# Seven block products for the first four heads' values and gates in a two-layer decoder trunk

## The chip, the core and the metric

The kernel runs on one core of a Trainium2 chip. The metric is the device time of one execution in microseconds (us); less is better. The core's engines run in parallel, each through its own instruction queue in order: TensorE (PE in the profile, with its weight loads PEld), VectorE (DVE), ScalarE (ACT), GpSimd (POOL), and SyncE (SP), which here issues the DMAs. Semaphores order them. PE multiplies a stationary 128x128 tile by a moving tile of up to 512 columns and accumulates in PSUM; the other engines move PSUM to SBUF.

## The reference

One sequence of 512 tokens, width 1024, two layers. Layer 0 mixes tokens with a Mamba-2 recurrence, layer 1 with HGRN2; each is followed by a squared-ReLU MLP (width 4096), layer norms, and a gated embedding. What this change touches is the input of the HGRN2 mixer, with 8 heads of 128 columns:

```python
q, fz, v, g = jnp.split(u @ w_in, 4, axis=-1)          # u: 512 x 1024, w_in: 1024 x 4096
...
o = rms_norm(o, norm_w).reshape(bsz, seq, D_MODEL) * jax.nn.silu(g)
```

`v` are the values that the recurrence carries, `g` the gates that scale its output. All is float32.

## The kernel before

Each float32 operand is split into a high part (rounded to fp32r, made by ACT) and a low part (the difference, made by DVE), and each product is three matmuls, `mm3` (lines 117 to 120): high x high, high x low, low x high. A weight block of 128x1024 comes by DMA into one of three `raw` buffers; `unit` and `split` (lines 101 to 115) make its two parts, in one of six slots each (`whi`, `wlo`). A new split can start only when the matmuls that read its slot are done.

Layer 0's MLP already uses block products with sums. Two operands are cut into 2x2 blocks, and seven products of sums of blocks stand for eight products of blocks (Winograd's form of Strassen's method). `weight_sums` (line 314) makes the four sums of weights on DVE, in eight buffers named `r`; `half_blocks` makes the sums on the other side; `block_product` (line 335) runs the seven products and drains them into `acc`.

After the MLP, `mlp_and_gate` multiplies the tokens by gate weights, chunk by chunk (4 chunks of 128 tokens, 2 halves of 512 columns), and adds the gated embedding. `turn` (line 441) then transposes each finished tile on PE, and its high and low parts go to `x_n`: ACT makes the high part (L449), DVE the low one (L450). The last tile's turn is left over in `late` and is run a little later. `x_n` is the transposed token matrix on which all of HGRN2's projections work.

The projections are made by generators. `vg(i)` (line 780) multiplies by the value and gate weights of heads 2i and 2i+1 (four weight blocks, 4 chunks x 8 x 3 = 96 matmuls of 512 columns) and drains to two `res` tiles, values and gates, from the pool `w4` (two buffers for each of the tags a and b). `qf(h)` makes query and forget gate of head h (48 matmuls). `background()` (line 839) strings them together, with `out0`, half of the output projection; every step of it is three matmuls and counts 0.65.

The recurrence `hcore` (line 877) runs for a pair of heads. It has seven levels, m = 0 to 6 (`half` = 1 to 64), each with small matmuls on PE (L897, L911, L918), then products on DVE (L931, L932) that the next level needs, and copies into the score tile on ACT (L954, L960); then transposes (L967) and a copy (L969), states (L976 to L980), outputs (L989, L991), norm and gate (L996 to L1002), and transposes (L1009). After each it yields a credit from `FILL`, and `fill` runs as many background steps as the credit pays, so that PE has work while the other engines compute. The last pair's credits are scaled by `LAST`. PE's order in this stage is as written; on the other engines and elsewhere a scheduler orders by priority, which `tc.high_priority(offset=...)` raises. What is left of the second output projection follows by the scheduler and can also be put between.

At the start of this stage the background runs 16 steps of `vg(0)`, the late turn in between, then `qf(0)` and `qf(1)`, and `AHEAD` pays for some more.

Of the kernel before, what the change touches and what calls it, by code (L numbers as in the profile page):

```python
# [29 lines left out]
SOON = 40  # L30
# [8 lines left out]
FIRST_V = 8  # L39
CONSTS = dict(ident=P, triu=P, eps=1, convw=96, convb=24, dskip=16, snw=16, dtc=2, hlb=8, hnw=1)  # L40


# [1 line left out]
def trunk(ctx: ExitStack, tc, a):  # L44
    nc = tc.nc
    pool = lambda name, bufs, **kw: ctx.enter_context(tc.tile_pool(name=name, bufs=bufs, **kw))
    cpool = pool("consts", 1)
    raws = pool("raws", RAWS)
    whip = pool("whip", 6)
    wlop = pool("wlop", 6)  # L50
    b8 = pool("b8", 9)
    accp = pool("accp", 1)
    w4 = pool("w4", 2)
    sm = pool("sm", 2)
    pad = pool("pad", 1)
    psj = pool("psj", 4, space=PSUM)
    pst = pool("pst", 1, space=PSUM)
    psy = pool("psy", 1, space=PSUM)
# [42 lines left out]
    def unit(src, lead=LEAD):  # L101
        n = src.shape[1]
        with tc.high_priority(offset=lead):
            raw = mk(raws, [P, 1024], "raw")
            nc.sync.dma_start(raw[:, :n], src)
        return split(raw[:, :n], lead)

    def split(f, lead=LEAD):
        n = f.shape[1]
        with tc.high_priority(offset=lead):  # L110
            hi = mk(whip, [P, 1024], "whi", F32R)
            nc.scalar.copy(hi[:, :n], f)  # L112
            lo = mk(wlop, [P, 1024], "wlo", F32R)
            nc.vector.tensor_sub(lo[:, :n], f, f32(hi[:, :n]))  # L114
        return hi, lo

    def mm3(out, sh, sl, mh, ml, start, stop, **kw):
        nc.tensor.matmul(out, sh, mh, start=start, stop=False, **kw)  # L118
        nc.tensor.matmul(out, sh, ml, start=False, stop=False, **kw)  # L119
        nc.tensor.matmul(out, sl, mh, start=False, stop=stop, **kw)  # L120
# [26 lines left out]
    with tc.high_priority(offset=FIRST):  # L147
        idle = tmp("sq", [P, T])
        nc.vector.memset(idle, 0.0)
        ps = bank(psm, "pm")  # L150
# [3 lines left out]
    x_s = Split(8)  # L154
    four = [(mk(whip, [P, 2, T], "whi", F32R), mk(wlop, [P, 2, T], "wlo", F32R)) for _ in range(4)]
    with tc.high_priority(offset=FIRST):
# [7 lines left out]
        for k in range(8):  # L164
            hi, lo = (v[:, k % 2, :] for v in four[k // 2])
# [145 lines left out]
        put("s1", a22)  # L311
        put("s4", a12)

    def weight_sums(w, lead):

        t = [[None, None] for _ in range(4)]

        def load(i, u, src):
            t[i][u] = tmp("r", [P, 1024])
            nc.sync.dma_start(t[i][u], src)  # L320

        with tc.high_priority(offset=lead):
            for u in range(2):
                load(0, u, w[0][1][u])
                load(2, u, w[1][1][u])
                nc.vector.tensor_sub(t[2][u], t[2][u], t[0][u])
                load(1, u, w[0][0][u])
                nc.vector.tensor_sub(t[0][u], t[0][u], t[1][u])
                nc.vector.tensor_add(t[1][u], t[2][u], t[1][u])
            for u in range(2):  # L330
                load(3, u, w[1][0][u])
                nc.vector.tensor_sub(t[3][u], t[3][u], t[1][u])
        return t

    def block_product(w, blk, lead, first, after=None, turns=None, sums=None):
# [49 lines left out]
    def mlp_and_gate(layer, h_s, last):  # L385
# [35 lines left out]
        for g, period in enumerate(PERIODS):  # L421
            if g < 4:
                tiles = hidden(g)
            if g > 0:
                if g == 4:
                    h_s, after, turned, sums = norm(2 * layer + 1)
# [6 lines left out]
                w = [[[w2[8 * g - 8 + 4 * i + 2 * j + u] for u in range(2)] for j in range(2)] for i in range(2)]  # L433
# [2 lines left out]
                next(tiles if op == "T" else products)  # L436

        x_n = None if last else Split(8)
        late = []

        def turn(h, c):

            sl = slice(c * P, (c + 1) * P)
            pt = bank(pst, "pt")
            for j in range(4):
                nc.tensor.transpose(pt[:, j * P : (j + 1) * P], acc[:, c, h * 512 + j * P : h * 512 + (j + 1) * P], ident)
            v = pt.rearrange("p (j t) -> p j t", j=4)
            hh = x_n.hi[h][:, :, sl]
            nc.scalar.copy(hh, v)  # L449
            nc.vector.tensor_sub(x_n.lo[h][:, :, sl], v, f32(hh))  # L450

        pps = {}
# [9 lines left out]
        for h in range(2):  # L462
            pu = unit(a[f"wp_{layer}"][h])
            gu = [unit(a[f"wg_{layer}"][4 * h + j]) for j in range(4)]
            for c in range(NCH):
                sl = slice(c * P, (c + 1) * P)
# [18 lines left out]
                for i in range(2 if end else 1):  # L485
# [7 lines left out]
                    d = acc[:, c, fs]  # L493
# [7 lines left out]
        return x_n, late  # L501

    ps = bank(psj, "pj")
# [23 lines left out]
    ab = row("xs")  # L529
# [220 lines left out]
    g, s, ss = outs.pop(0)  # L750
    ssd_out(g, s, rms_group(ss), *after)
    begin("mlp0")
    x_s, late = mlp_and_gate(0, h_s, False)
# [26 lines left out]
    def vg(i):  # L780


        pss = {}
        units = []
        res = [mk(w4, [P, NCH, 256], "ab"[which]) for which in range(2)]
        for j, c in ((j, c) for j in range(4) for c in range(NCH)) if i else ((j, c) for c in range(NCH) for j in range(4)):
            if j == len(units):
                units.append(unit(a["whvg"][4 * i + j]))
            if j == 0:
                pss[c] = bank(psj, "pj")  # L790
            hi, lo = units[j]
            sl = slice(c * P, (c + 1) * P)
            for k in range(2):
                ks = slice(k * 512, (k + 1) * 512)
                x = x_s.h(2 * j + k, sl), x_s.l(2 * j + k, sl)
                mm3(pss[c], *x, hi[:, ks], lo[:, ks], j + k == 0, j == 3 and k == 1)
                yield 0.65
            if j == 3:
                for which in range(2):
                    nc.scalar.copy(res[which][:, c, :], pss[c][:, 256 * which : 256 * (which + 1)])  # L800
        nc.scalar.activation(res[1], res[1], AF.Silu)
        made["vg", i] = res

    def qf(h):
# [48 lines left out]
    made = {}  # L853
# [23 lines left out]
    def hcore(h0, s, i0):  # L877

        R = range(2)
        base = lambda half: 0 if half == 32 else 128  # L880
        vs = [slice(r * P, (r + 1) * P) for r in R]
# [82 lines left out]
        for r in R:  # L964
# [3 lines left out]
            kt.append(tmp("btok", [P, 3, P]))  # L968
            nc.scalar.copy(kt[r], pt[:, : 3 * P].rearrange("p (c k) -> p c k", c=3))  # L969
            yield FILL[1]  # L970
        v, sg = need("vg", h0 // 2)
        sv = []
        for r in R:
            pss = py(1) if r else bank(psm, "pm")
            for c in range(3):
                nc.tensor.matmul(pss[:, c * P : (c + 1) * P], kt[r][:, c, :], v[:, c, vs[r]], start=True, stop=True)  # L976
            sv.append(tmp("pv", [P, 3, P]))
            nc.scalar.copy(sv[r][:, 0], pss[:, 0:P])
            for c in range(1, 3):
                nc.vector.scalar_tensor_tensor(  # L980
                    sv[r][:, c], sv[r][:, c - 1], tot[r][:, c : c + 1], pss[:, c * P : (c + 1) * P], ALU.mult, ALU.add
                )
            yield FILL[2]
        os = []
        for r in R:
            po = py(r)
            for c in range(NCH):
                sl = slice(c * P, (c + 1) * P)
                nc.tensor.matmul(po[:, sl], scs[r][:, c, :], v[:, c, vs[r]], start=True, stop=c == 0)  # L989
                if c:  # L990
                    nc.tensor.matmul(po[:, sl], qd[r][:, sl], sv[r][:, c - 1, :], start=False, stop=True)  # L991

            ms = mk(sm, [P, NCH], "hms")
            o = tmp("cbm", [P, NCH, P])
            for c in range(NCH):
                nc.scalar.activation(o[:, c, :], po[:, c * P : (c + 1) * P], AF.Square, accum_out=ms[:, c : c + 1])  # L996
            nc.scalar.activation(ms, ms, AF.Sqrt, scale=1.0 / P, bias=eps)
            ri = mk(sm, [P, NCH], "hri")
            nc.vector.reciprocal(ri, ms)
            for c in range(NCH):  # L1000
                nc.vector.scalar_tensor_tensor(
                    o[:, c, :], po[:, c * P : (c + 1) * P], ri[:, c : c + 1], sg[:, c, vs[r]], ALU.mult, ALU.mult  # L1002
                )
            os.append(o)
            yield FILL[3]
# [144 lines left out]
```

## Time and profile before

| | us |
|---|---|
| median of 3 runs (lowest, highest) | 1431.18 (1430.93, 1432.43) |
| span of the profiled execution | 1430.3 |
| PE, PEld busy in it | 1422.1, 1180.6 |
| DVE, ACT, POOL busy in it | 1011.7, 735.0, 1.9 |

The profile is of one execution; its own time is not listed beside the runs, and its span is what lies between its first and last instruction, 0.9 under the median. A row of the timeline gives start and length in us, engine, line and operation, the tile written and the tiles read, shapes, and in brackets the idle time before it and what ended that. A row of a group gives count, busy time in all, mean in ns of one, and idle time before with its releasers. A matmul's length is pipelined and modelled, so its cost is read from the distance of the starts.

In the profiled execution the MLP of layer 0 ends at some 705 us, the gated embedding at some 766, and the first level of the recurrence begins at 807.7; its last level starts at 1000.1.

### The profile page before, as it was taken

To read this page: it belongs to the slowest core of one execution; us is meant where nothing else is said; L and a number is where in the kernel's file an instruction comes from. 1 tells how busy PE (TensorE), PEld (TensorE's weight loads), DVE (VectorE), ACT (ScalarE), POOL (GpSimd) and SP (SyncE) were. 2 spreads that over 40 slices of the span, in tenths; PEclk is the share of its full clock that TensorE was granted. 3 is DMA by queue.
4 is the path that set the end of the run, shared out by engine and by line. 5 is a ranking of instruction groups with operands and counts; after the bars stand their busy time and mean duration, and the time that the engine had idled before them with its cause. 6 is when DMAs were issued, how large, how long until landed. Compare 5 with 4: busy or idle time off the path is not lost.

```text
span 1430.3 us, 20978 instructions
## 1 busy us (share of the span) xinstructions
PE 1422.1 (99%) x8405; PEld 1180.6 (83%) x8405; DVE 1011.7 (71%) x1636; ACT 735.0 (51%) x1113; POOL 1.9 (0%) x12
## 2 busy tenths in 40 slices
PE   9999999999999999999999999999999999999998
PEld 7788888888888888888888887887898888888887
DVE  7988687797967667687853555556685867667873
ACT  6776454563264444545533465554555454544641
POOL 0000000000000000000000000000000000000000
PEclk9999999999999999999999999999999999999999
DMA  8332323233333444442422322122163434434231
GB/s 305 133 131 91 119 88 120 102 117 127 140 118 133 147 143 138 147 135 101 162 77 74 119 75 89 62 88 96 49 232 113 147 132 148 146 133 162 89 118 44
DMA packets 48529, 174.88 MB, mean 122 GB/s; under 512 B 5424, under 2 KB 6192, under 8 KB 48304
## 3 DMA queue, kind: packets, MB, share of 16 engines
q1 hardware_dynamic: 48432, 173.55, 34.8%
q8 instruction: 66, 1.08, 0.3%
q14 instruction: 31, 0.25, 0.1%
HBM read 171.36 MB, written 2.16 MB: 121 GB/s over the span
## 4 chain that ended last, share of the span: by engine, by line
PE 96%; DVE 2%; ACT 1%; DMA 0%; issue 0%; SPq 0%; DVEq 0%; ACTq 0%
PE pj L118 25%; PE pj L119 24%; PE pj L120 24%; PE py L118 5%; PE py L119 5%; PE py L120 5%; PE py L674 1%; PE py L680 1%; PE pm L644 1%; PE py L911 1%; PE pt L232 1%; DVE wlo L114 1%; PE pt L632 1%; PE py L989 0%; DMA r<-in_w 0%; PE py L991 0%
## 5 line engine op out<-in xcount | busy, mean ns | idle before, releaser
L112 ACT CAST whi<-raw 128x1024 fp32r<-128x1024 f32 x224 | 234.9, 1051 | 340.1 <-PE pj L119 240.0
L118 PE MATMUL pj<-b,whi 128*128 128x512 f32 (+1 forms) x1006 | 382.6, 381 | 0.7 <-ACT b L236 0.7
L119 PE MATMUL pj<-b,whi 128*128 128x512 f32 (+1 forms) x1006 | 381.0, 379 | 0.5 <-DVE b L237 0.5
L114 DVE TENSOR_TENSOR wlo<-raw,whi 128x1024 fp32r<-128x1024 f32 x224 | 272.5, 1222 | 153.4 <-ACT whi L112 150.5
L120 PE MATMUL pj<-b,wlo 128*128 128x512 f32 (+1 forms) x1006 | 379.7, 378 | 0.0
L118 PE MATMUL pj<-whi,b 128*128 128x512 f32 x576 | 230.1, 400 | 0.0
L120 PE MATMUL pj<-whi,b 128*128 128x512 f32 x584 | 228.7, 392 | 0.0
L119 PE MATMUL pj<-wlo,b 128*128 128x512 f32 x576 | 226.1, 393 | 0.0
L118 PEld LDWEIGHTS pj<-b,whi 128*128 128x128 f32 x1006 | 189.2, 188 | 34.3 <-ACT b L236 0.9
L119 PEld LDWEIGHTS pj<-b,whi 128*128 128x128 f32 x1006 | 189.8, 189 | 33.4 <-issue 0.9
L120 PEld LDWEIGHTS pj<-b,wlo 128*128 128x128 f32 x1006 | 189.6, 189 | 33.4
L120 PEld LDWEIGHTS pj<-whi,b 128*128 128x128 f32 x584 | 109.7, 188 | 22.5
L118 PEld LDWEIGHTS pj<-whi,b 128*128 128x128 f32 x576 | 108.4, 188 | 21.6 <-ACT b L1010 0.6
L119 PEld LDWEIGHTS pj<-wlo,b 128*128 128x128 f32 x576 | 108.5, 188 | 20.2
L112 ACT CAST whi<-r 128x1024 fp32r<-128x1024 f32 x64 | 67.4, 1054 | 63.7 <-PE pj L120 35.6
L114 DVE TENSOR_TENSOR wlo<-r,whi 128x1024 fp32r<-128x1024 f32 x64 | 78.1, 1221 | 21.6 <-ACT whi L112 21.4
L120 PE MATMUL py<-whi,b 128*128 128x512 f32 (+1 forms) x218 | 84.6, 388 | 0.0
L119 PE MATMUL py<-wlo,b 128*128 128x512 f32 x192 | 74.8, 390 | 0.0
L118 PE MATMUL py<-whi,b 128*128 128x512 f32 x192 | 74.5, 390 | 0.0
L573 DVE SCALAR_TENSOR_TENSOR cv<-pj,cst,cv 128x509 f32<-128x509 f32 (+2 forms) x66 | 48.7, 745 | 3.5 <-ACT cv L570 2.8
L120 PEld LDWEIGHTS py<-whi,b 128*128 128x128 f32 x218 | 41.0, 188 | 8.4
L931 DVE TENSOR_TENSOR cv<-cv,y 128x256 f32<-128x256 f32 x48 | 20.2, 422 | 33.0 <-PE py L911 20.4
(260 smaller groups left out, 1809.6 us busy)
## 6 DMA issues: line engine op xcount, KB each, us to landing
raw<-in_w SPq DMA_DIRECT2D x112, 512.0 KB, 3.2
r<-in_w SPq DMA_DIRECT2D x64, 512.0 KB, 3.4
raw<-in_wssd SPq DMA_DIRECT2D x36, 512.0 KB, 3.4
a<-csd SPq DMA_DIRECT2D x16, 512.0 KB, 3.7
raw<-in_wso SPq DMA_DIRECT2D x16, 512.0 KB, 3.2
raw<-in_wg SPq DMA_DIRECT2D x16, 512.0 KB, 3.3
raw<-in_whvg SPq DMA_DIRECT2D x16, 512.0 KB, 3.3
raw<-in_whq SPq DMA_DIRECT2D x16, 512.0 KB, 3.3
```

Source lines behind the costliest of these rows:

```text
L112: nc.scalar.copy(hi[:, :n], f)
L114: nc.vector.tensor_sub(lo[:, :n], f, f32(hi[:, :n]))
L118: nc.tensor.matmul(out, sh, mh, start=start, stop=False, **kw)
L119: nc.tensor.matmul(out, sh, ml, start=False, stop=False, **kw)
L120: nc.tensor.matmul(out, sl, mh, start=False, stop=stop, **kw)
L232: nc.tensor.transpose(pt[:, j * P : (j + 1) * P], src[:, k * P : (k + 1) * P], ident)
L573: nc.vector.scalar_tensor_tensor(cv[:, d:], ps[:, : T - d], convw[:, i, k : k + 1], cv[:, d:], ALU.mult, ALU.add)
L632: nc.tensor.transpose(pt[:, c * P : (c + 1) * P], xs[:, c * P : (c + 1) * P], ident)
L644: nc.tensor.matmul(pst_[:, c * P : (c + 1) * P], btok[:, c, :], xw[:, c].rearrange("p h q -> p (h q)"), start=True, stop=True)
L674: nc.tensor.matmul(yd[64 * r : 64 * r + 64, sl], xdt[:, 2 * c + r, :], m[:, r, sl], start=True, stop=True)
L680: nc.tensor.matmul(yo[:, c * P : (c + 1) * P], pv[:, c - 1].rearrange("p h q -> p (h q)"), cm[:, c * P : (c + 1) * P], start=True, stop=True,)
L931: nc.vector.tensor_mul(kv[:, :, 0, :], kv[:, :, 0, :], bc(tv[:, :, 1], 2, half))
```

## The change

The values and gates of heads 0 to 3 (`vg(0)` and `vg(1)`) are no longer made in the background. A new function, `values4`, makes them in one go directly after the gated embedding, with seven block products: tokens 0 to 255 and 256 to 511 by the two halves of the 1024 inner columns on one side, the same inner halves by heads 0 and 1 and heads 2 and 3 on the other. Each product is 2 chunks x 4 x 3 = 24 matmuls.

- The sums of weights come from `weight_sums`, now with an engine as argument: GpSimd here, with priority raised by 300, so that its loads and sums are placed early, towards the end of the MLP. Eight loads and eight operations of 128x1024. Six more weight blocks are loaded again and used as they are.
- The sums of transposed tokens need the tokens in float32: `turn` copies each transposed tile once more on ACT, into `rows`. DVE forms four sums, and each is split (`put`) into high and low parts in a `b8` buffer.
- The order of the products is: part (0,0); [late turn]; part (0,1); s3 with the third weight sum; s2 with the second; part (1,1) with the fourth; s1 with the first; s4. "Product three" below is the one on s3. The drains are copies on ACT (`first`) or additions on DVE (`more`).
- The background loses `vg(0)` and `vg(1)`; the credits in `FILL` are scaled down; `res` tiles now hold values and gates of two chunks each; the mask's load goes to a `raw` buffer in place of a `w4` one.

```diff
-JOBS = "q2 q3 v1 q4 q5 v2 q6 q7 v3 o".split()
-FILL = (3.7, 1.3, 1.6, 2.3, 2.8)
+JOBS = "q2 q3 q4 q5 v2 q6 q7 v3 o".split()
+FILL = (3.15, 1.1, 1.35, 1.95, 2.4)
+VALUE_SUMS = 300
...
-    def weight_sums(w, lead):
+    def weight_sums(w, lead, eng=nc.vector):
...
-                nc.vector.tensor_sub(t[2][u], t[2][u], t[0][u])
+                eng.tensor_sub(t[2][u], t[2][u], t[0][u])
...
         x_n = None if last else Split(8)
+        rows = None if last else [tmp("blk", [P, 2, 4, 256]) for _ in range(2)]
...
             nc.scalar.copy(hh, v)
+            nc.scalar.copy(rows[c // 2][:, h, :, c % 2 * P : (c % 2 + 1) * P], v)
             nc.vector.tensor_sub(x_n.lo[h][:, :, sl], v, f32(hh))
...
+    def values4(xs, rows, late):
+
+        w = [[[a["whvg"][4 * j + 2 * i + u] for u in range(2)] for j in range(2)] for i in range(2)]
+        t1, t2, t3, t4 = weight_sums(w, VALUE_SUMS, nc.gpsimd)
+        a11, a12, a21, a22 = (rows[i][:, j] for i in range(2) for j in range(2))
+        res = [[mk(w4, [P, 2, T], "ab"[i]) for i in range(2)] for _ in range(2)]
+
+        def put(f):
+            t = mk(b8, [P, 2, 4, 256], "b8", F32R)
+            nc.scalar.copy(t[:, 0], f)
+            nc.vector.tensor_sub(t[:, 1], f, f32(t[:, 0]))
+            return lambda k, c: tuple(t[:, i, k, c * P : (c + 1) * P] for i in range(2))
...
+        def product(x, us, banks, start, drain):
+            for c in range(2):
+                for k in range(4):
+                    hi, lo = us[k // 2]
+                    ks = slice(k % 2 * T, (k % 2 + 1) * T)
+                    mm3(banks[c], *x(k, c), hi[:, ks], lo[:, ks], start and k == 0, k == 3, skip_group_check=True)
+                with tc.high_priority(offset=SOON):
+                    drain(c, banks[c])
...
+        product(part(0, 0), [unit(v) for v in w[0][0]], x, True, first(0, 0))
+        for f in late:
+            f()
+        nc.vector.tensor_add(a22, a21, a22)
+        nc.vector.tensor_sub(a21, a11, a21)
+        s3 = put(a21)
+        product(part(0, 1), [unit(v) for v in w[1][0]], z, True, more(0, 0))
+        nc.vector.tensor_sub(a11, a22, a11)
+        s2 = put(a11)
+        product(s3, sums(t3), y, True, first(1, 1))
+        product(s2, sums(t2), x, False, first(1, 0))
+        s1 = put(a22)
+        product(part(1, 1), sums(t4), y, False, more(1, 0))
+        nc.vector.tensor_sub(a12, a12, a11)
+        s4 = put(a12)
+        product(s1, sums(t1), x, False, more(1, 1))
+        product(s4, [unit(v) for v in w[1][1]], x, False, first(0, 1))
+        for j in range(2):
+            for i in range(2):
+                g = res[j][i][:, :, 256:]
+                nc.scalar.activation(g, g, AF.Silu)
+            made["vg", j] = res[j]
...
+    with tc.manual_schedule(engines={mybir.EngineType.PE}):
+        values4(x_s, rows, late)
     begin("hgrn")
...
-    lmf = mk(w4, [P, 6, 32], "a")
+    lmf = mk(raws, [P, 1024], "raw")[:, :192].rearrange("p (m l) -> p m l", m=6)
...
-        first = vg(0)
-        for _ in range(FIRST_V):
-            yield next(first)
-        for f in late:
-            f()
-        for _ in range(FIRST_V):
-            yield next(first)
         yield from qf(0)
         yield from qf(1)
-        yield from first
```

More of the change, by code (lines that the diff above doesn't have):

```diff
@@ L33 @@
 SUMS = (60, 300, 300, 300)
-JOBS = "q2 q3 v1 q4 q5 v2 q6 q7 v3 o".split()
-FILL = (3.7, 1.3, 1.6, 2.3, 2.8)
+JOBS = "q2 q3 q4 q5 v2 q6 q7 v3 o".split()
+FILL = (3.15, 1.1, 1.35, 1.95, 2.4)
+VALUE_SUMS = 300
 AHEAD = 6.0
 LAST = 0.78
-FIRST_V = 8
 CONSTS = dict(ident=P, triu=P, eps=1, convw=96, convb=24, dskip=16, snw=16, dtc=2, hlb=8, hnw=1)
@@ L325, in weight_sums @@
                 load(2, u, w[1][1][u])
-                nc.vector.tensor_sub(t[2][u], t[2][u], t[0][u])
+                eng.tensor_sub(t[2][u], t[2][u], t[0][u])
                 load(1, u, w[0][0][u])
-                nc.vector.tensor_sub(t[0][u], t[0][u], t[1][u])
-                nc.vector.tensor_add(t[1][u], t[2][u], t[1][u])
+                eng.tensor_sub(t[0][u], t[0][u], t[1][u])
+                eng.tensor_add(t[1][u], t[2][u], t[1][u])
             for u in range(2):
                 load(3, u, w[1][0][u])
-                nc.vector.tensor_sub(t[3][u], t[3][u], t[1][u])
+                eng.tensor_sub(t[3][u], t[3][u], t[1][u])
         return t
@@ L500, in mlp_and_gate, with part, first, more @@
                     late.append(lambda h=h, c=c: turn(h, c))
-        return x_n, late
+        return x_n, rows, late
+    def values4(xs, rows, late):
[8 more added lines that the diff above has]
+            return lambda k, c: tuple(t[:, i, k, c * P : (c + 1) * P] for i in range(2))
+        def part(i, j):
+            sl = lambda c: slice((2 * i + c) * P, (2 * i + c + 1) * P)
+            return lambda k, c: (xs.h(4 * j + k, sl(c)), xs.l(4 * j + k, sl(c)))
+        def product(x, us, banks, start, drain):
[6 more added lines that the diff above has]
+                    drain(c, banks[c])
+        def first(i, j):
+            return lambda c, ps: nc.scalar.copy(res[j][i][:, c], ps)
+        def more(i, j):
+            return lambda c, ps: nc.vector.tensor_add(res[j][i][:, c], ps, res[j][i][:, c])
+        pair = lambda: [bank(psj, "pj") for _ in range(2)]
+        sums = lambda t: [split(v) for v in t]
+        x, z, y = [bank(psy, "py%d" % c) for c in range(2)], pair(), pair()
+        product(part(0, 0), [unit(v) for v in w[0][0]], x, True, first(0, 0))
[20 more added lines that the diff above has]
+            made["vg", j] = res[j]
@@ L752, in trunk @@
     begin("mlp0")
-    x_s, late = mlp_and_gate(0, h_s, False)
+    x_s, rows, late = mlp_and_gate(0, h_s, False)
+    made = {}
+    with tc.manual_schedule(engines={mybir.EngineType.PE}):
+        values4(x_s, rows, late)
     begin("hgrn")
     lmask = mk(cpool, [P, 6, 32], "lmask", U8)
-    lmf = mk(w4, [P, 6, 32], "a")
+    lmf = mk(raws, [P, 1024], "raw")[:, :192].rearrange("p (m l) -> p m l", m=6)
     nc.sync.dma_start(lmf, a["lmask"])
@@ L784, in vg @@
         units = []
-        res = [mk(w4, [P, NCH, 256], "ab"[which]) for which in range(2)]
-        for j, c in ((j, c) for j in range(4) for c in range(NCH)) if i else ((j, c) for c in range(NCH) for j in range(4)):
+        res = [mk(w4, [P, 2, T], "ab"[half]) for half in range(2)]
+        for j, c in ((j, c) for j in range(4) for c in range(NCH)):
             if j == len(units):
@@ L798, in vg @@
             if j == 3:
-                for which in range(2):
-                    nc.scalar.copy(res[which][:, c, :], pss[c][:, 256 * which : 256 * (which + 1)])
-        nc.scalar.activation(res[1], res[1], AF.Silu)
+                nc.scalar.copy(res[c // 2][:, c % 2], pss[c])
+        for r in res:
+            nc.scalar.activation(r[:, :, 256:], r[:, :, 256:], AF.Silu)
         made["vg", i] = res
@@ L839, in background @@
     def background():
-        first = vg(0)
-        for _ in range(FIRST_V):
-            yield next(first)
-        for f in late:
-            f()
-        for _ in range(FIRST_V):
-            yield next(first)
         yield from qf(0)
         yield from qf(1)
-        yield from first
         for job in JOBS:
             yield from {"v": vg, "q": qf}[job[0]](int(job[1])) if job != "o" else out0()
-    made = {}
     bg = background()
@@ L880, in hcore @@
         base = lambda half: 0 if half == 32 else 128
-        vs = [slice(r * P, (r + 1) * P) for r in R]
         q, f, kk = ([need("qf", h0 + r)[n] for r in R] for n in range(3))
@@ L970, in hcore @@
             yield FILL[1]
-        v, sg = need("vg", h0 // 2)
+        res = need("vg", h0 // 2)
+        v = lambda c, r: res[c // 2][:, c % 2, r * P : (r + 1) * P]
+        sg = lambda c, r: res[c // 2][:, c % 2, 256 + r * P : 256 + (r + 1) * P]
         sv = []
@@ L975, in hcore @@
             for c in range(3):
-                nc.tensor.matmul(pss[:, c * P : (c + 1) * P], kt[r][:, c, :], v[:, c, vs[r]], start=True, stop=True)
+                nc.tensor.matmul(pss[:, c * P : (c + 1) * P], kt[r][:, c, :], v(c, r), start=True, stop=True)
             sv.append(tmp("pv", [P, 3, P]))
@@ L988, in hcore @@
                 sl = slice(c * P, (c + 1) * P)
-                nc.tensor.matmul(po[:, sl], scs[r][:, c, :], v[:, c, vs[r]], start=True, stop=c == 0)
+                nc.tensor.matmul(po[:, sl], scs[r][:, c, :], v(c, r), start=True, stop=c == 0)
                 if c:
@@ L1001, in hcore @@
                 nc.vector.scalar_tensor_tensor(
-                    o[:, c, :], po[:, c * P : (c + 1) * P], ri[:, c : c + 1], sg[:, c, vs[r]], ALU.mult, ALU.mult
+                    o[:, c, :], po[:, c * P : (c + 1) * P], ri[:, c : c + 1], sg(c, r), ALU.mult, ALU.mult
                 )
```

## The prediction

> **What bounds the kernel now.** I read the page first: its first part, then the chain that ended last. TensorE (PE) has work in 1422.1 of 1430.3 us, and 96% of the chain is PE.
>
> ```profile
> span 1430.3 us, 20978 instructions
> PE 1422.1 (99%) x8405; PEld 1180.6 (83%) x8405; DVE 1011.7 (71%) x1636; ACT 735.0 (51%) x1113; POOL 1.9 (0%) x12
> ...
> PE 96%; DVE 2%; ACT 1%; DMA 0%; issue 0%; SPq 0%; DVEq 0%; ACTq 0%
> ```
>
> So the time is the sum of PE's instructions plus its waits: a removed matmul counts in full, and so does a new wait of PE. Next comes the timeline of PE where the changed stage begins. (Columns: start, length, engine, line.) These rows are the second and the last of the 24 matmuls ahead of the last turned tile, the four transposes, and the next matmul.
>
> ```profile
> 767.15 0.39 PE L119 MATMUL pj<-wlo,b 128*128 128x512 f32 x1
> ...
> 772.16 0.39 PE L120 MATMUL pj<-whi,b 128*128 128x512 f32 x1
> 772.39 0.60 PE L446 MATMUL pt<-cst,acc 128*128 128x128 f32 x4
> 772.75 0.48 PE L118 MATMUL pj<-whi,b 128*128 128x512 f32 x1
> ```
>
> A row's length, 0.39, is pipelined; what a 128x512 matmul costs is the distance of starts: 22 steps in 5.01 us, 0.228 each. For the other engines I take the groups by shape (mean ns of one behind the bar), and one hand-over from PE to ACT to DVE:
>
> ```profile
> L112 ACT CAST whi<-raw 128x1024 fp32r<-128x1024 f32 x224 | 234.9, 1051 | 340.1 <-PE pj L119 240.0 <-PE pj L120 72.0 <-PE py L120 20.7
> L114 DVE TENSOR_TENSOR wlo<-raw,whi 128x1024 fp32r<-128x1024 f32 x224 | 272.5, 1222 | 153.4 <-ACT whi L112 150.5 <-DMA r<-in_w 2.0
> L332 DVE TENSOR_TENSOR r<-r,r 128x1024 f32<-128x1024 f32 x16 | 19.6, 1222 | 7.7 <-DMA r<-in_w 7.6
> L365 DVE TENSOR_TENSOR acc<-py,acc 128x512 f32<-128x512 f32 x44 | 30.1, 687 | 6.5 <-PE py L120 6.5
> L449 ACT CAST b<-pt 128x512 fp32r<-128x512 f32 x8 | 4.7, 585 | 1.5 <-PE pt L446 1.5
> L800 ACT COPY a<-pj 128x256 f32<-128x256 f32 x16 | 6.0, 372 | 20.0 <-PE pj L120 20.0
> ```
>
> ```profile
> 758.98 0.39 PE L120 MATMUL pj<-whi,b 128*128 128x512 f32 x1
> 759.40 0.60 ACT L484 ACTIVATE sg<-pj 128x512 f32<-128x512 f32 x1 [6.20 <-PE pj L120]
> 760.04 0.69 DVE L491 TENSOR_TENSOR sg<-py,sg 128x512 f32<-128x512 f32 x1 [5.39 <-ACT sg L484]
> ```
>
> ACT starts 0.42 after the start of PE's last matmul, DVE 0.04 after ACT's end.
>
> **The change, part by part.**
>
> *Removed on PE.* Eight block products' worth, 192 matmuls, become 7 x 24 = 168. 24 x 0.228 = 5.5 us off the path.
>
> *Work beside PE.* ACT: six more weight splits and four block copies at 1.05, eight row copies at 0.585 (L449's shape), eight drains at some 0.59 in place of 32 at 0.37 (L800): 10.5 + 4.7 + 4.7 - 11.8 = 8 us more at most. DVE: ten operations more for weights and blocks (lo parts), four sums of tokens, six drains: 14 x 1.22 + 6 x 0.69 = 21 us. Neither is bound over the whole span, but both now stand ahead of PE inside one stage of 38 us.
>
> *The wait ahead of the third product.* I follow the changed program's order on each engine. PE runs product one from 766.83, the late transposes at 772.39, product two from 772.75 (last matmul starts at 772.75 + 0.32 + 22 x 0.228 = 778.1), so product three, on token sums, is due at 778.3. On ACT its hi copy stands behind the splits of the fourth weight sum. Those write the two of six slots that product two reads; the second can start only 0.42 after its last matmul: 778.5. Then 1.05 (split) and 1.05 (hi copy): PE's first matmul comes at 780.65, 2.3 late. On DVE the order is: both token sums, two lo parts of those weights, a drain, and then product three's lo part. The second lo part begins at 779.6; 1.13 + 0.6 + 1.22 later product three's lo is there, 782.6 to 783.1 (the later if the token sums, whose input is turned at about 776, hold DVE until 779). Product three's third matmul reads it, due 778.8: PE is 3.9 to 4.4 late. I take 4.2. No row of before shows such a wait; as bounds, 2.3 (ACT alone) and 5.4 (one more 1.22 in front on DVE).
> Next late would be product four: its block sum, copy and lo part end 3.5 after product three's lo, its turn comes 22 x 0.228 = 5.0 after. Covered with 1.5; a table load and a SiLU stand on ACT in that gap.
>
> *Levels of the recurrence.* Each level of a head pair gets 15 matmuls beside it, where 18 stood.
>
> ```profile
> 817.08 0.74 PE L911 MATMUL py<-qd,cv 128*32 128x16 f32 x64
> 817.61 0.43 DVE L931 TENSOR_TENSOR cv<-cv,y 128x256 f32<-128x256 f32 x1 [1.70 <-PE py L911]
> 818.62 0.42 DVE L932 TENSOR_TENSOR qd<-qd,y 128x256 f32<-128x256 f32 x1
> 822.08 0.74 PE L911 MATMUL py<-qd,cv 128*32 128x16 f32 x64
> 980.88 0.74 PE L911 MATMUL py<-qd,cv 128*32 128x16 f32 x64
> 984.51 0.74 PE L911 MATMUL py<-qd,cv 128*32 128x16 f32 x64
> ```
>
> A level took 5.0 and will take 4.3; DVE's chain ends 2.0 after PE's start, 3.2 with a split in front, and the last pair already ran at 3.63 without a wait. Cost 0; were the cover gone, 1 us a level.
>
> *The last head pair.* The filler ends in it. Between its level-32 matmuls and its last transposes PE's order has 30 filler matmuls, where 63 stood.
>
> ```profile
> 994.58 2.46 ACT L954 COPY sc<-scb 32x128 f32<-32x128 f32 x8 [0.97 <-DVE scb L946]
> 996.07 0.46 PE L918 MATMUL py<-qd,cv 128*32 128x32 f32 x32
> 998.02 1.71 ACT L960 COPY sc<-py 32x64 f32<-32x64 f32 x8
> 1000.08 0.69 PE L918 MATMUL py<-qd,cv 128*64 128x64 f32 x16
> 1004.09 0.48 ACT L969 COPY btok<-pt 128x384 f32<-128x384 f32 x1 [2.43 <-PE pt L967]
> 1017.66 0.60 PE L1009 MATMUL pt<-cst,cbm 128*128 128x128 f32 x4
> ```
>
> Now from level 32 at t: ACT's 16 copies run from t to t + 4.2 (2.46 + 1.71), and level 64's second half waits for them, due at t + 3.45: 0.75. Then a weight split (1.05) and four copies stand ahead of the token copy (0.48): 0.65. The states and the norm add some 0.5. That is 1.9; from 996.07 to 1018.0 before needed 21.95 - 63 x 0.228 = 7.6 without filler, of which some 0.5 are such waits. I take 1.4; bounds 0 and 3.
>
> *Weight sums on POOL.* Eight additions and subtractions of 128x1024, early: their inputs are loaded as the buffers of the last MLP block product's sums come free. POOL's rows are memsets; the others show who waits for DVE at that place (the last is a stretch: us, PE, PEld, DVE, ACT, POOL busy, clock, DMA).
>
> ```profile
> L766 POOL MEMSET sc<- 128x512 f32 x2 | 1.0, 530 | 674.5 <-PE pj L120 674.5
> ```
>
> ```profile
> r<-in_w SPq DMA_DIRECT2D x64, 512.0 KB, 3.4
> ```
>
> ```profile
> 662.74 1.23 DVE L114 TENSOR_TENSOR wlo<-r,whi 128x1024 fp32r<-128x1024 f32 x1 [3.01 <-ACT whi L112]
> 671.13 0.69 DVE L300 TENSOR_TENSOR blk<-a,blk 128x512 fp32r<-128x512 f32 x1
> 671.88 0.49 PE L120 MATMUL pj<-whi,blk 128*128 128x512 f32 x1
> 674.13 1.29 DVE L365 TENSOR_TENSOR acc<-py,acc 128x512 f32<-128x512 f32 x2
> 675.39 0.63 PE L118 MATMUL py<-whi,b 128*128 128x512 f32 x2
> ```
>
> ```profile
> 664.00:676.60 12.60, 12.60 (x57) 10.22 (x56) 11.96 (x17) 9.45 (x13) 0.99 (x3) 1.00 0.13 42
> ```
>
> DVE is busy 11.96 of 12.6 us there and PE follows it closely: L300's lo part ends at 671.82 and PE's matmul starts at 671.88; L365's pair ends at 675.42 and the second matmul of 675.39's pair is PE's next. So what delays DVE here delays PE one to one. The second load is issued at 664.0, lands 3.4 later, and three of POOL's eight operations begin between 667.4 and some 674. One lasts between 1.06 (two memsets of 530) and 3.2 (a pass for each of three operands); I take 2.1, a pass for each input. Whether POOL's reading holds up DVE, no row shows: the memsets, beside L114, did not, but they read nothing. Bounds: 0, and three in full, 3 x 3.2 = 9.5 (a gain is excluded: DVE loses no work here). I take two of the three standing ahead of DVE, since each arrives within a running DVE operation and can follow it, and the third falling beside L365, whose first input is in PSUM: 2 x 2.1 - 0.1 = 4.1. The other five, after 680, I take as 0: their price is the next cover, DVE's idle time behind 676.6.
> [...]
>
> *Loads.* Six more of 512 KB, eight of the stage's fourteen on SP ahead of the MLP's last two weights. The last of them waits for a split that stands on DVE just ahead of the one that the next load waited for before: 0 on the path; the mask's load, moved behind six weights, follows a split that ends at about 766.3 and lands 1.9 later, by its row; DVE reaches the cast behind product one's tail at about 770.9.
>
> ```profile
> a<-in_lmask SPq DMA_DIRECT2D x1, 96.0 KB, 1.9
> ```
>
> *Sum* against the profiled execution: 1430.3 - 5.5 + 4.2 + 1.4 + 4.1 = 1434.5. The median of the runs stands 0.9 above that span (1431.18), so 1435.4.
>
> **The rivals.**
> 1. *POOL costs nothing.* For it: the memset beside L114. Against it: the memset reads nothing. 1431.18 - 5.5 + 4.2 + 1.4 = 1431.3, no change that can be told (a measurement here tells about 0.2%, 2.9 us).
> 2. *Strict turns.* All eight POOL operations hold DVE for their length: three give 6.2 in the stretch above, and the five later ones displace DVE work that PE waits for up to its idle time; another 2. 1431.18 + 0.1 + 8.2 = 1439.5. [...] Against it: POOL may wait for DVE as often as DVE for POOL.
> 3. *Faster.* The wait ahead of product three shrinks: its place is ACT's queue behind the two splits, its price 4.2. With POOL free it decides once it is under 1.2 us; at 0 the time is 1427.1. Against it: the six slots and the order are fixed in the program.
> 4. *The clock falls.* PE stands still for 2.3 and 1.9 us with two matmuls between. The longest idle time of PE so far is its start's, with the clock at 1.00 as in the stretch above:
>
> ```profile
> PE pm L152 <- DVE sq L149: 1.4, 1, 1.4
> ```
>
> At half clock the 24 matmuls of product three take 5.5 more: 1440.9. [...]
>
> **How the numbers follow.** Forecast 0.38, rival one 0.33, two 0.15, three 0.09, four 0.05. Forecast, two and four are slower by over 0.2%, 0.58, less some 0.04 where POOL's delay stays under 2.8; rival one lies within, save 0.02 on either side. So slower 0.56, same 0.33, faster 0.11. The range reaches from three's upper part, 1428.5, to just over two, 1440.5; the forecast's own is 1433 to 1438.
>
> **What would show it.** After: 5442 in place of 5466 matmuls of 512 columns; PE waiting for ACT and then DVE just after product two, 2 and 2 us, in the chain; PE waits on the token copy and states of the last pair; between 667 and 680 POOL's operations of about 2 us, DVE rows of 0.69 or 1.22 lengthened beside them, and PE following late. The forecast is wrong if DVE's rows there keep their lengths (rival one), if PE has no wait at product three (three), or if PE's clock column falls (four). If POOL's operations are far longer than 3.2, even two of them cost more than the upper bound.

## The result, and the profile after

The change makes the kernel slower: 1454.57 us (median of 4 runs, 1454.22 to 1456.57) against 1431.38 of the kernel before on the same chip, a ratio of 1.0163 with a 95% interval of 1.0149 to 1.0178. The range that I gave ended at 1440.5. The profiled execution has a span of 1452.5, 22.2 more than before.

The page of the changed kernel, its first part and its chain:

```profile
span 1452.5 us, 20985 instructions
PE 1424.6 (98%) x8381; PEld 1177.8 (81%) x8381; DVE 1046.4 (72%) x1656; ACT 745.5 (51%) x1117; POOL 27.3 (2%) x20
...
PE 90%; DVE 5%; ACT 3%; DMA 1%; issue 1%; ACTq 0%; DVEq 0%
```

The 24 matmuls are gone (8405 to 8381), yet the chain is PE to 90% only, where it was 96%. PE's waits by releaser (us in total, times, longest) are:

```profile
PE pj L120 <- DVE blk L300: 5.6, 1, 5.6
PE pt L232 <- DVE acc L223: 3.6, 1, 3.6
PE pt L1063 <- DVE b L1065: 2.3, 1, 2.3
PE pj L118 <- ACT b L514: 2.1, 1, 2.1
PE pj L120 <- DVE b L515: 1.7, 1, 1.7
...
PE pt L1019 <- ACT btok L1021: 1.4, 2, 0.8
...
PE py L970 <- ACT sc L1012: 1.2, 3, 0.5
```

To place the loss I compare the starts of the same matmuls. Timeline of PE, before, then after (the last row of after answers to the one at 772.39 in the prediction, the second to the one at 675.39):

```profile
661.68 0.39 PE L118 MATMUL py<-whi,blk 128*128 128x512 f32 x1
694.44 0.39 PE L118 MATMUL pj<-whi,b 128*128 128x512 f32 x1
705.33 0.60 PE L232 MATMUL pt<-cst,acc 128*128 128x128 f32 x4
```

```profile
661.11 0.39 PE L118 MATMUL py<-whi,blk 128*128 128x512 f32 x1
684.18 0.62 PE L118 MATMUL py<-whi,b 128*128 128x512 f32 x2
705.31 0.39 PE L118 MATMUL pj<-whi,b 128*128 128x512 f32 x1
719.95 0.66 PE L232 MATMUL pt<-cst,acc 128*128 128x128 f32 x4 [3.60 <-DVE acc L223]
787.30 0.60 PE L447 MATMUL pt<-cst,acc 128*128 128x128 f32 x4
```

After is 0.57 ahead at 661; 8.79 behind at 684.18; 10.87 at 705.31; 14.62 at 719.95; 14.91 at the late turn. So the stretch in which GpSimd forms the sums of weights costs 9.4, then 2.1, then 3.7 us (the norm comes late), 15.5 in all with 0.3 in the embedding. What GpSimd and DVE do there (timeline rows of both, after; below them the first two of these DVE rows before, the third is the one at 671.13 in the prediction):

```profile
666.73 3.24 POOL L326 TENSOR_TENSOR r<-r,r 128x1024 f32<-128x1024 f32 x1 [665.62 <-DMA r<-in_whvg]
671.15 3.30 POOL L328 TENSOR_TENSOR r<-r,r 128x1024 f32<-128x1024 f32 x1 [1.18 <-DVE blk L300]
674.53 2.67 POOL L329 TENSOR_TENSOR r<-r,r 128x1024 f32<-128x1024 f32 x1
```

```profile
667.62 2.89 DVE L306 TENSOR_TENSOR a<-a 128x512 f32<-128x512 f32 x1
672.17 2.82 DVE L307 TENSOR_TENSOR a<-b,a 128x512 f32<-128x512 f32 x1
674.92 2.83 DVE L300 TENSOR_TENSOR blk<-a,blk 128x512 fp32r<-128x512 f32 x1
691.68 3.43 DVE L432 TENSOR_TENSOR b<-raw,a 128x1024 fp32r<-128x1024 f32 x1
695.04 0.68 DVE L365 TENSOR_TENSOR acc<-pj,acc 128x512 f32<-128x512 f32 x1
```

```profile
668.19 0.68 DVE L306 TENSOR_TENSOR a<-a 128x512 f32<-128x512 f32 x1
670.53 0.69 DVE L307 TENSOR_TENSOR a<-b,a 128x512 f32<-128x512 f32 x1
```

Each of the first three sums lengthens one DVE row of 0.68 to 0.69 to 2.8 or 2.9, by 2.13 to 2.21, 6.5 in all; the last of these rows is the lo part for which PE waits 5.6. The other five lengthen five rows between 688 and 705 by 0.98 to 2.21, 8.0 in all (the one at 691.68 took 1.22 before). The sums are longer as well: one takes 2.40 alone (below) and up to 3.30 here. The row at 695.04 runs inside a GpSimd sum too (694.11 to 697.35) and keeps its 0.68; its first input is in PSUM. So do the other four DVE rows with an input in PSUM that run inside sums, at 688.34, 695.64, 701.70 and 702.30, of 0.67 to 0.68.

PE then stands at half clock (0.50). Stretches of the changed kernel (us; busy us of PE, PEld, DVE, ACT, POOL; granted clock; DMA share, GB/s):

```profile
670.28:673.69 3.41, 1.48 (x6) 0.57 (x4) 3.41 (x4) 0.62 (x1) 2.54 (x1) 1.00 0.47 132
673.69:683.93 10.24, 6.13 (x14) 4.79 (x15) 8.47 (x9) 3.31 (x4) 3.43 (x2) 0.50 0.21 60
714.65:718.06 3.41, 1.70 (x8) 1.08 (x6) 3.41 (x6) 2.70 (x5) 0.00 (x0) 1.00 0.29 91
718.06:721.47 3.41, 1.52 (x9) 1.35 (x10) 3.41 (x6) 1.43 (x3) 0.00 (x0) 1.00 0.84 273
793.16:796.57 3.41, 0.94 (x3) 0.30 (x2) 3.41 (x4) 3.10 (x3) 0.00 (x0) 1.00 0.00 0
796.57:803.40 6.83, 5.47 (x13) 4.32 (x14) 5.94 (x6) 3.59 (x6) 0.00 (x0) 0.50 0.00 0
```

From PE's restart at 677.80 to 683.93 a matmul takes nearly twice as long (0.43 from start to start, where it is 0.228 before): of the 9.4 us some 2.9 are this, and 6.5 the DVE rows above. The second half-clock stretch falls on product three:

```profile
795.49 0.50 PE L118 MATMUL pj<-whi,b 128*128 128x512 f32 x1 [2.13 <-ACT b L514]
797.93 0.80 PE L120 MATMUL pj<-whi,b 128*128 128x512 f32 x1 [1.71 <-DVE b L515]
803.54 0.39 PE L118 MATMUL pj<-whi,b 128*128 128x512 f32 x1
```

Without a wait it would have begun at 793.21 (PE's last matmul ahead of it starts at 792.98), and its sixteenth matmul at 793.21 + 15 x 0.227 = 796.61; it starts at 803.54, 6.9 late: 3.8 of recorded waits, the rest nearly all half clock. Behind that the recurrence has 4.9 us of waits: 1.2 on score copies, 1.4 on token copies, 2.3 ahead of one pair's transposes. The sum: -0.6 (the start) + 15.5 - 5.5 + 6.9 + 4.9 = 21.2 of 22.2; 1 us is spread and not accounted for.

### The profile page after: what moved, and what is told of

Its sections match the earlier page's. It is cut to its first block, busy times and chain, and to the rows that moved or that the text cites. A ratio compares the mean times of both kernels' runs of the same rounds, so it can differ in the third digit from the quotient of the medians.

```text
span 1452.5 us, 20985 instructions
## 1 busy us (share of the span) xinstructions
PE 1424.6 (98%) x8381; PEld 1177.8 (81%) x8381; DVE 1046.4 (72%) x1656; ACT 745.5 (51%) x1117; POOL 27.3 (2%) x20
## 4 chain that ended last, share of the span: by engine, by line
PE 90%; DVE 5%; ACT 3%; DMA 1%; issue 1%; ACTq 0%; DVEq 0%
PE pj L118 23%; PE pj L120 23%; PE pj L119 23%; PE py L118 4%; PE py L119 4%; PE py L120 4%; DVE wlo L114 2%; PE py L733 1%; DMA raw<-in_wssd 1%; PE pt L232 1%; PE py L739 1%; PE pm L703 1%; PE py L963 1%; ACT whi L112 1%; PE pt L691 1%
## 5 line engine op out<-in xcount | busy, mean ns | idle before, releaser
L118 PE MATMUL pj<-whi,b 128*128 128x512 f32 x536 | 214.7, 401 | 2.7 <-ACT b L514 2.1
L120 PE MATMUL pj<-whi,b 128*128 128x512 f32 x544 | 214.2, 395 | 1.7 <-DVE b L515 1.7
L119 PE MATMUL pj<-wlo,b 128*128 128x512 f32 x536 | 211.2, 394 | 0.0
L120 PEld LDWEIGHTS pj<-whi,b 128*128 128x128 f32 x544 | 102.8, 189 | 23.4 <-DVE b L515 2.1
L118 PEld LDWEIGHTS pj<-whi,b 128*128 128x128 f32 x536 | 101.4, 189 | 24.2 <-ACT b L514 2.5
L119 PEld LDWEIGHTS pj<-wlo,b 128*128 128x128 f32 x536 | 101.4, 189 | 19.5
L112 ACT CAST whi<-r 128x1024 fp32r<-128x1024 f32 x72 | 75.8, 1053 | 71.3 <-PE pj L120 40.1
L114 DVE TENSOR_TENSOR wlo<-r,whi 128x1024 fp32r<-128x1024 f32 x72 | 89.4, 1242 | 26.6 <-ACT whi L112 26.2
L120 PE MATMUL py<-whi,b 128*128 128x512 f32 (+1 forms) x250 | 97.0, 388 | 0.0
L118 PE MATMUL py<-whi,b 128*128 128x512 f32 x224 | 87.2, 391 | 0.9 <-DVE acc L365 0.9
L119 PE MATMUL py<-wlo,b 128*128 128x512 f32 x224 | 87.2, 389 | 0.0
L120 PEld LDWEIGHTS py<-whi,b 128*128 128x128 f32 x250 | 46.9, 188 | 9.7
L118 PEld LDWEIGHTS py<-whi,b 128*128 128x128 f32 x224 | 42.1, 188 | 10.5 <-DVE acc L365 1.4
```

## The experiments

**Does GpSimd's reading hold up DVE?** Two kernels keep everything of the change, but leave out the sums: GpSimd writes a constant, or copies one operand, in place of each.

```diff
+    class Marks:
+        def tensor_sub(self, out, x, y):
+            nc.gpsimd.memset(out, 0.5)          # second kernel: nc.gpsimd.tensor_copy(out, x)
+        tensor_add = tensor_sub
...
-        t1, t2, t3, t4 = weight_sums(w, VALUE_SUMS, nc.gpsimd)
+        t1, t2, t3, t4 = weight_sums(w, VALUE_SUMS, Marks())
```

> The eight sums of weights on GpSimd are replaced by eight memsets of the same tiles, which read nothing; loads, waits and order stay. (Part of the computation is left out: the products work on constants in place of the four sums.) Theory one, GpSimd's reading of two operands holds up VectorE: rows of VectorE between 667 and 705 keep 0.69 and 1.22, TensorE has none of its five waits there, the clock stays at 1.00, and the time is 1454.6 less 9.4, 2.1 and 3.7 = 1439.4. Rival, the loads or GpSimd's writing do it: VectorE's rows stay at 2.8, time 1450 to 1455.

Measured: 1438.56, so 16.0 less than the change. Between 655 and 720 PE has no wait, and the clock is 1.00. Rows of GpSimd and DVE (the edit moves DVE's drain from L365 to L372, the half-block lines stay):

```profile
666.74 0.96 POOL L317 MEMSET r<- 128x1024 f32 x1 [3.10 <-DMA r<-in_whvg]
...
667.67 0.68 DVE L306 TENSOR_TENSOR a<-a 128x512 f32<-128x512 f32 x1
670.01 0.68 DVE L307 TENSOR_TENSOR a<-b,a 128x512 f32<-128x512 f32 x1
```

The loads are the same, and the first three are issued at the same time (from 659.23; 659.19 in the change); it is the reading of the sums that costs 15 to 16 us. From the matmul at 661 to the late turn PE takes 110.90 here, 126.19 in the change and 110.72 before: 15.3. The rest of the 16.0 is mostly the clock at product three, where the half clock lasts 3.41 us here and 6.83 in the change (68.46 and 69.42 from the late turn to the first level). DVE's busy time is 14.5 us less than in the change (1031.9 and 1046.4), the 6.5 and 8.0 of the rows above. So the DVE rows with two SBUF inputs had 2.13 to 2.21 added by each of the first three sums, which read SBUF, and nothing beside a memset, which only writes it.

> The eight sums become copies on GpSimd with one operand read from SBUF instead of two (the sums are left out of the computation). If every reading operation of GpSimd holds VectorE for its length, the delay of each scales with that length: rows of VectorE lengthened by some 1.1 to 2.2, time 1445 to 1454. If only two-operand operations do it, VectorE's rows keep 0.69 and 1.22 and the time is that of the memsets, 1439.4.

Measured: 1442.43, between the two expectations. A copy lengthens a DVE row by up to 0.85, less than I had thought, and PE waits 1.5 in place of 5.6:

```profile
666.62 1.53 DVE L306 TENSOR_TENSOR a<-a 128x512 f32<-128x512 f32 x1
670.41 1.52 DVE L300 TENSOR_TENSOR blk<-a,blk 128x512 fp32r<-128x512 f32 x1
...
674.96 1.04 POOL L317 COPY r<-r 128x1024 f32<-128x1024 f32 x1 [3.58 <-DVE acc L372]
```

So with one operand read DVE's rows are longer too, and in these two sizes what it costs goes with GpSimd's own length: a copy beside drains takes 1.04 and adds up to 0.85, a sum without DVE takes 2.40 (below) and adds up to 2.21. With a wait of 1.5 us PE kept its full clock there (1.00 from 660 to 720). From 661 to the late turn the eight copies cost 2.1 more than the memsets (113.03 and 110.90), the eight sums 15.3. The medians are 3.9 apart because the clock differs elsewhere: 6.83 us of half clock at product three where the memsets' profile has 3.41, and 3.41 behind a 2.3 us wait of the recurrence where it has none.

**The same sums on VectorE.**

```diff
-        t1, t2, t3, t4 = weight_sums(w, VALUE_SUMS, nc.gpsimd)
+        t1, t2, t3, t4 = weight_sums(w, VALUE_SUMS)
```

> The eight sums go to VectorE, at 1.22 us each, 9.8 in all. The scheduler, which then sees them compete for VectorE, puts none of them ahead of the MLP's last sums and drains, but between the norm's steps and after. Theory one: the waits of 9.4 and 2.1 go; the norm may come late by up to the three sums ahead of it less the idle time there, 0 to 3: 1439.4 to 1442.5, I take 1440.5. Rival, VectorE is short of time in this stretch whoever forms the sums: TensorE waits for VectorE nearly as before, 1448 or more.

Measured: 1440.18, as expected (1440.5), 14.4 under the change. No wait on DVE is left between 655 and 720. From 661 to the late turn it takes 110.75, no more than with memsets; so the number came out by luck, since 1.1 of it stood for a norm that comes late. The 1.6 above the memsets are the clock again (the profiled spans are 2.1 apart): 6.83 us of half clock at product three in place of 3.41 cost 1.2 (69.63 and 68.46 from the late turn to the first level), and a stretch of half clock behind the 2.3 us wait of the recurrence, which in the profiles of the change and of the memsets kept the full clock, costs 1.4 (53.87 and 52.44 for the second pair):

```profile
941.97:945.38 3.41, 3.11 (x10) 2.63 (x11) 0.99 (x2) 0.69 (x1) 0.00 (x0) 0.50 0.00 0
```

So 9.8 us of sums cost next to nothing on the busy engine, and 15 on the idle one. On DVE they stand in one queue with the MLP's rows: the first begins at 686.57, behind the last of L365's sums, and the next ones between the steps of the norm. GpSimd's queue holds nothing else there, and its first and fourth sums start as their loads land (666.73 and 687.65), the first in the middle of the sums on which PE waits. That the scheduler weighs the one and not the other is my reading of this order; no run shows its reasons.

**The token sum for product three.**

```diff
+        d = mk(raws, [P, 1024], "raw").rearrange("p (k t) -> p k t", k=4)
+        nc.vector.tensor_sub(d, a11, a21)
+        s3 = put(d)
         product(part(0, 0), [unit(v) for v in w[0][0]], x, True, first(0, 0))
...
-        nc.vector.tensor_sub(a21, a11, a21)
-        s3 = put(a21)
```

> The token sum for product three is formed in a buffer of its own ahead of product one (it needs no late tile), in place of over one of its operands after the late turn. Theory: the 2.1 and 1.7 us waits ahead of product three go, and with them the half clock of its first 13 matmuls; 793.21 + 15 x 0.227 = 796.6 in place of 803.5, so 6.9 less: 1447.7. Rival: product four or the split of the third sum comes late in its place (ACT's and VectorE's queues stay as full): a wait of 1 to 4 us one product on, 1449 to 1453.

Measured: 1449.93, 4.6 less in place of 6.9. At the place itself the theory holds: no wait of PE is left from 780 to 812, and from the late turn to the first level of the recurrence it takes 62.44 in place of 69.42, 7.0 less. The change, then the experiment:

```profile
856.72 0.89 PE L949 MATMUL py<-xs,cv 128*32 128x48 f32 x64
```

```profile
788.25 0.60 PE L447 MATMUL pt<-cst,acc 128*128 128x128 f32 x4
850.69 0.89 PE L950 MATMUL py<-xs,cv 128*32 128x48 f32 x64
```

The rest is lost elsewhere: the 3.6 us wait ahead of the norm's transposes, at full clock in the change, is followed by half clock here, and so is the 2.3 us wait of the recurrence (clock 0.59 from 952 to 954; 1.5 for the second pair, 53.95 in place of 52.45). From the norm's transposes to the late turn it takes 68.87 in place of 67.35, and the late turn is 1.06 later against the start of the stretch (661.00 here, 661.11 in the change):

```profile
719.38 0.66 PE L232 MATMUL pt<-cst,acc 128*128 128x128 f32 x4 [3.61 <-DVE acc L223]
...
719.00:722.00 3.00, 2.62 (x10) 2.21 (x11) 3.00 (x4) 1.53 (x2) 0.00 (x0) 0.71 0.52 178
```

**Both together, and the credits.** The last two edits in one kernel, and then the same with the credit of a level changed:

```diff
-FILL = (3.15, 1.1, 1.35, 1.95, 2.4)
+FILL = (2.9, 1.1, 1.35, 1.95, 2.4)      # the third kernel: 3.0
```

> Sums of weights on VectorE and the early sum for product three together. Theory: the waits ahead of the norm (15.2 in all) and ahead of product three (6.9) go, what is left of the change is 24 matmuls less, -5.5, and the waits of the recurrence, +4.9, with up to 1.5 for the clock where the 2.3 us wait falls badly: 1431 to 1433, I take 1431.7, no change against the kernel before. Rival, the two causes share one cost (VectorE's backlog): less than the sum of both gains, 1436 or more.

> As before this one, and the credit of a level is 2.9 in place of 3.15, so that each level gets one matmul triple less now and then, more is left for the last head pair, and the drain of a query and gate projection falls elsewhere on ScalarE. Theory: the second pair's 2.3 us wait on the transposes' bank is a matter of what stands ahead on ScalarE there, and goes; the waits on score copies stay: 1428 to 1430, I take 1428.9. Rival, levels get too short for VectorE's chain: waits at each level, 1431 to 1436.

> As the first, with a level's credit at 3.0. Here the copy out of the transposes' bank stands ahead of the projection's drain on ScalarE as well. Theory: the same as at 2.9, 1428 to 1430.5. If the wait is one of too little work and not of the order on ScalarE, it stays at some 2 us: 1431.7.

Measured: 1433.35 with both (ratio to before 1.0006, 0.9997 to 1.0015): 1440.2 less the 7.0 at product three, so the two causes are separate, and 1.6 above the 1431.7 that I had. With 2.9: 1432.64 (1.0004, 0.9996 to 1.0013), outside my 1428 to 1430; with 3.0: 1430.58 (0.9991, 0.9983 to 1.0000), at the end of mine. The wait ahead of the second pair's transposes does go with either credit, but a like one comes up in the third pair, where the drains and gates of a value projection now stand ahead on ScalarE. At 2.9 it is 2.2 and half clock follows (0.63 from 980 to 984), at 3.0 it is 1.8 and none does (1.00 from 976 to 984). PE's second transposes of these two pairs, at 3.0, then the gate and the copy out of the first bank that it holds up on ScalarE:

```profile
929.95 0.60 PE L1064 MATMUL pt<-cst,cbm 128*128 128x128 f32 x4
...
980.38 0.63 PE L1064 MATMUL pt<-cst,cbm 128*128 128x128 f32 x4 [1.78 <-DVE b L1066]
```

```profile
975.96 0.63 ACT L864 ACTIVATE b<-b 128x512 f32<-128x512 f32 x1
978.11 0.67 ACT L1065 ACTIVATE b<-pt,cst 128x512 fp32r<-128x512 f32 x1
```

So half of the theory stands: it is the order on ScalarE, and a credit only shifts where the two meet. The first transposes of that pair had begun at 975.26; table loads of 1.28 stand on both sides of the gate.

**GpSimd at a quieter place.** With the early token sum, the loads of GpSimd's sums wait for the first gated tile of tokens.

```diff
             t[i][u] = tmp("r", [P, 1024])
+            if gate is not None:
+                nc.gpsimd.tensor_copy(t[i][u][:, :1], gate)      # gate: acc[:, 0, 0:1]
```

> Sums on GpSimd again, but their loads wait for the first gated token tile (a one-column copy into each buffer), so that they run from some 745 us on, in the gated embedding, where VectorE is busy about half of the time; with the early sum for product three. Theory: GpSimd still holds VectorE's rows by some 2.2 us, eight times, but TensorE does not wait for them there: as the first of these, 1431 to 1434. Rival, weight splits and gates come late in the embedding: TensorE waits, 1436 to 1445.

Measured: 1438.2, 4.9 above the kernel with both edits; the rival is right. The sums run from 728 to 751, earlier than I had meant. Alone, one takes 2.40; and where DVE splits weights (wlo) or adds gates (acc) beside them, PE waits again, 3.5 in all (DVE rows of 3.40 at 742.39 and 1.67 at 746.91, of 1.21 and 0.68 without a sum beside them); 1.4 more is half clock behind the recurrence's 2.3 us wait in this profile (0.62 from 940 to 944):

```profile
727.89 2.40 POOL L328 TENSOR_TENSOR r<-r,r 128x1024 f32<-128x1024 f32 x1 [4.59 <-DMA r<-in_whvg]
...
745.85 0.50 PE L119 MATMUL pj<-wlo,b 128*128 128x512 f32 x1 [1.67 <-DVE wlo L114]
748.73 0.63 PE L449 MATMUL pt<-cst,acc 128*128 128x128 f32 x4 [1.46 <-DVE acc L498]
```

**A second bank for the transposes.** The transposes of a pair's second head wait until the first head's bank is read; here they get another.

```diff
-            pt = bank(pst, "pt")
+            pt = bank(psm, "pm") if r else bank(pst, "pt")
             for c in range(NCH):
                 nc.tensor.transpose(pt[:, c * P : (c + 1) * P], os[r][:, c, :], ident)
```

> As the kernel with sums on VectorE and the early sum for product three, and the second head's transposes of a pair go to the other small PSUM bank, so that they need not wait until ScalarE and VectorE have read the first head's. Theory: the 2.3 us wait ahead of the second pair's transposes is for the bank alone and goes: 1433.4 less 2.3 = 1431.1, lower by up to 1.5 more where the clock fell on that wait in some runs. Rival, the same queue on ScalarE only moves the wait to the next user of its result: 1433.

> The same with a level's credit of 3.0. Its wait for the bank was 1.8: 1430.6 less 1.8 = 1428.8, or 1430.5 by the rival. Against the kernel before, 0.2 per cent faster by the theory.

Measured: 1429.53 (0.9983, 0.9974 to 0.9992) and, with a level's credit of 3.0, 1428.78 (0.9978, 0.9969 to 0.9987): as the theory had it. With a bank of its own the second head's transposes have no wait for ScalarE in either profile. The longest of PE's waits behind the embedding in the second kernel is now:

```profile
PE pt L1020 <- DVE cv L984: 0.9, 1, 0.9
```

This is the version that beats both: 3.4 us under the kernel before on its chip (1432.15), of the 5.5 that the matmuls are worth.

## Why the prediction was wrong, point by point

- **Removed on PE, -5.5.** Right in count; and the last kernel shows 3.4 of it as time; the rest I put down to the waits that remain.
- **The wait ahead of the third product, +4.2.** The wait itself was right: first ACT's hi copy, 2.1 (expected 2.3), then DVE's lo part, 1.7, together 3.8; and product four followed without one. What failed is that the term held the wait only: half clock made it 6.9. I had that as rival four, with 0.05, and priced it at 24 slow matmuls; 13 were, 3 us. That the clock would go to half was my assumption, which no row of before shows; after, it is 0.50 there.
- **Levels of the recurrence, 0.** The levels' own chain is covered, as said. But I looked only there: two score copies came late by 0.9 in the first pair, a token copy by 0.6 and a bank by 2.3 in the second. The filler had shifted, so that a projection's drain stood on ScalarE just where the bank was to be emptied. The step left out that fewer filler matmuls also move where the drains fall.
- **The last head pair, +1.4.** The waits in it are 1.0, near, but in part by luck: score copies 0.26 where I had 0.75, the token copy 0.78 where I had 0.65, none at the states and the norm where I had 0.5; and the 0.5 that I took off for before stands in none of its waits.
- **Weight sums on POOL, +4.1.** This is the step that failed: 15 to 16. GpSimd's length was near (2.1 taken, 2.40 alone; DVE is held 2.13 to 2.21). But I counted two of three ahead of DVE, expecting the third to fall beside L365, whose first input is in PSUM. That such a row stays free was my assumption, which no row of before shows; L365 is indeed free of it after (0.68 at 695.04), yet with DVE already 4.3 late the third sum met a lo part instead. Then "the other five, after 680, I take as 0": PE lost another 5.8 to them, as DVE's backlog reached the norm. And the 5.6 us of idle PE brought half clock, 2.9. My bound of 9.5 was three lengths, and left out the other five and the clock, so it was no bound. Rival two (strict turns) had the mechanism, 6.2 here and 2 later; measured are 6.5 and 5.8.
- **Loads, 0.** Right: with memsets the same loads cost nothing.

## What to carry to other kernels

Work moved to GpSimd was not free where VectorE was busy: in these runs a sum (2.40 alone) lengthened VectorE rows with two SBUF inputs by 0.98 to 2.21, a copy by up to 0.85 and a memset by nothing, and rows with an input in PSUM kept 0.67 to 0.68 inside a sum; so eight sums of 1.22 us on VectorE became eight delays of 1.0 to 2.2, 14.5 in all. Count every delay on the stretch, not only the first, and follow the backlog to the next thing that PE waits for. Price the half clock behind a wait of PE too: in these profiles it followed the wait of 5.6 us and some of those of 2.1 to 3.6, with 1.4 to 3 us lost at the places measured above, and the clock stayed at 1.00 behind the 1.5 us of the copies and the 1.8 at a credit of 3.0.

## What the runs showed of the hardware that I had not expected

In the profile of the change the clock went to 0.50 and back at whole multiples of one length: in the rows above the half-clock stretches are 10.24 and 6.83 us long, three and two times 3.413, and their beginnings, 673.69 and 796.57, are 122.88 apart, 36 times 3.413. The two falls follow stretches of 3.41 us in which PE had 1.48 and 0.94 us of work; after 1.70 and 1.52 us of work, in the two stretches that share the 3.6 us wait, the clock stayed. The 2.3 us wait of the recurrence shows the same, here with the sums on VectorE and then with both edits; half clock follows the first (the row at 941.97 above) and not the second:

```profile
938.56:941.97 3.41, 1.41 (x7) 0.83 (x5) 0.85 (x2) 2.87 (x5) 0.00 (x0) 1.00 0.48 154
933.57:936.98 3.41, 1.58 (x9) 1.42 (x10) 0.92 (x2) 1.68 (x3) 0.00 (x0) 1.00 0.31 125
```

So a 3.6 us wait cost no clock in the change and 1.5 us in the experiment with the early token sum, where the stretches lie elsewhere (half clock from some 720.3, by the clock of 0.57 between 720 and 722); a 2.3 us wait kept the full clock in the profile of the change and lost 1.4 with the sums on VectorE. In the profiles of all twelve kernels the clock falls twelve times ahead of their last matmuls, each time behind such a stretch with 0.00 to 1.48 us of PE's work; the least work shown here after which it stayed at 1.00 is 1.52, then 1.58, counted as the profile models matmuls.
